# Norm sums inside the first FFN tile, and more Strassen tiles in layer 0

## The chip, the core and the metric

The kernel runs on one core of a Trainium2 chip. The metric is the device time of one execution in microseconds (us). A core has several engines that work side by side, each through its own queue, in order: PE (TensorE, matrix products), DVE (VectorE), ACT (ScalarE), POOL (GpSimd), and SP, which here issues nearly all loads. PE writes into PSUM, the others read it; operands lie in SBUF, in 128 partitions.

## The reference

A decoder trunk of two layers over 512 tokens with a model width of 1024. Each layer has a mixer, a cross-attention into 256 memory tokens, and a SwiGLU FFN of width 2816, each with an RMS norm before it and a residual add behind it. The change is in the FFN:

```python
def rms_norm(x, g):
    y = xf * lax.rsqrt(jnp.mean(xf * xf, axis=-1, keepdims=True) + RMS_EPS)
    return (y * g).astype(x.dtype)

def swiglu(h, w_gate_up, w_down):
    g, u = jnp.split(h @ w_gate_up, 2, axis=-1)
    return (jax.nn.silu(g) * u) @ w_down

x = x + swiglu(rms_norm(x, ffn_norm[layer]), ffn_w_gate_up[layer], ffn_w_down[layer])
```

## The kernel before

**Layout and precision.** Activations lie transposed: features in the partitions, the 512 tokens (T) along the free axis; a 1024-wide activation is eight such tiles (KD = 8). Float32 accuracy comes from splitting each operand into a high and a low part (`split`, L156 on ACT for the high part, L157 on DVE for the low; with a per-feature gain L159 and L160). A product is three matmuls, high by high, high by low and low by high (`mm3`, L169 to L171). Weights come in raw blocks by DMA (L93) and are split on ACT (L101) and DVE (L102); there are two raw buffers and three each of high and low.

**The FFN** (`ffn`) goes through the 2816 hidden features in 22 tiles f0 to f21 of 128, in parts of 4, 4, 4, 4 and 6 tiles. A *plain* tile makes its gate and up products with 48 matmuls of 512 columns (8 feature tiles x 3 x 2). A *fast* tile uses a Strassen form over two halves of the features and two halves of the tokens: seven products of 4 feature tiles, 84 matmuls of 256 columns. It needs sums and differences of half tiles of the normed features (`TA`, `TB`; L797 to L800, split into `ta` and `tb`) and sums of weight blocks, made by DVE from raw blocks `gr` and split into `sw`. f4 to f15 are fast in both layers. The down products of a part (8 of them, 12 matmuls each) run two per tile during the next part; those of the last part follow at the end. Gate and up of a plain tile go to the PSUM banks `mm` and `att`, sums and broadcasts to `tr`, down products to `s`; each has two buffers.

**The norm at the FFN's front.** During the cross-attention's output projection every finished tile of x is scaled by the norm's gain and split (`xg`), and its square is added to `ssq` on POOL (L250). The first two tiles f0 and f1 take `xg`, that is features without the norm's factor. Then four times two small matmuls with a column of ones sum `ssq` over the features (L186, `rstd_cols`); a short chain on DVE (L195, L220 to L223) and POOL (L219) makes the reciprocal root, DVE spreads it over a diagonal (L231), one matmul broadcasts it to all partitions (L233) and ACT copies it to R (L239). f0 and f1 are multiplied by R behind their products (L890, L892). From f2 on the products take the normed features `xn` = x times gain times R (L791), split by L156 and L157. In the code `normed` makes two of these, their half sums and the splits of both, four times.

**Last part and key scaling.** Before f16 the pool of the fast tiles is closed, and its memory is free for others. In layer 0, `aside` runs behind f17: it scales and splits the keys of the memory for the next layer (`mg`, eight times L159 on ACT and L160 on DVE).

**Order.** The program is written in the order of the code, and a scheduler then decides for each engine the order of its instructions, from a timing model and the dependences. `tc.issue_after(ins)` adds an order without a wait: what is inside comes behind `ins` on its engine.

Of the kernel before, what the change touches and what calls it, by code (L numbers as in the profile page):

```python
# [9 lines left out]
F32 = mybir.dt.float32  # L10
F32R = mybir.dt.float32r
# [3 lines left out]
ALU = mybir.AluOpType  # L15
# [3 lines left out]
P = 128  # L19
T = 512  # L20
D = 1024
KD = D // P
NT = T // P
# [9 lines left out]
DFF = 2816  # L33
NF = DFF // P
FFN_PARTS = (4, 4, 4, 4, 6)
FAST = range(4, 16)
HT = T // 2
KH = KD // 2
WARM = 12
EPS = 1e-6  # L40
PADW = 16
# [65 lines left out]
class Trunk:  # L107
# [128 lines left out]
    def norm_row(self, ssq, dim):  # L236
        ps = self.bcast(self.rstd_cols((ssq, dim, NT, None))[0])
        R = self.rp.tile([P, T], F32, name=self.nm("R"), tag="R")
        self.nc.scalar.copy(R, ps)  # L239
        return R  # L240

# [15 lines left out]
        return {"side": side, "gain": gain, "off": off, "ssq": self.new_ssq(), "xg": []}  # L257

    def feed(self, nxt, m, x=None):
        x = self.x[m] if x is None else x  # L260
        if nxt["gain"] is not None:
            h, l = self.pair(nxt["side"])
            self.split(x, h, l, scale=self.vec(nxt["gain"], nxt["off"] + m))
            nxt["xg"].append((h, l))
        self.add_square(nxt["ssq"], x, m == 0)

    def linear(self, W, blk, xs, off=0, bank="mm", ps=None, k0=0, k1=None):

# [163 lines left out]
    def even(self, nrm, nxt_spec):  # L432
# [4 lines left out]
        with ExitStack() as ctx:  # L437
# [20 lines left out]
            nc.scalar.activation(sq[2], z[2], AF.Square)  # L458
            R = self.rp.tile([P, T], F32, name=self.nm("R"), tag="R")
            ups = [self.linear(Win, 0, xg, bank="s", k1=3)]  # L460
# [4 lines left out]
            with tc.issue_after(self.mm_ins):  # L465
                row = self.bcast(rx)
            nc.scalar.copy(R, row)
            Rk = self.tmp("t1")
# [6 lines left out]
            kr = self.tmp("t0")  # L475
            nc.vector.tensor_mul(kr[rr], z[3][rr], R[rr])
            ta, tb = self.tmp("t1"), self.tmp("t1")
# [283 lines left out]
    def ffn(self, layer, nrm, nxt_spec, aside=None):  # L761


        nc, ins = self.nc, self.ins
        xg, A = nrm["xg"], nrm["side"]
        B = 1 - A
        final = nxt_spec is None
# [4 lines left out]
        Wg = Weights(self, ins["ffn_gu"], f"gu{layer}")  # L772
        lo, hi = slice(0, HT), slice(HT, T)
        xn, TA, TB = [None] * KD, [], []

        def products(f, xs):
            pg = self.linear(Wg, (layer * NF + f) * 2, xs, bank="mm")
            return pg, self.linear(Wg, (layer * NF + f) * 2 + 1, xs, bank="att")

        def hidden(u):  # L780
            h, l = self.pair(A)
            self.split(u, h, l)
            return h, l

        def normed(st):

            for k in range(KH):
                g = []
                for m in (k, k + KH):
                    t = self.inp.tile([P, T + PADW], F32, name=self.nm("xn"), tag="in")[:, :T]  # L790
                    nc.vector.scalar_tensor_tensor(t, self.x[m], self.vec(nrm["gain"], nrm["off"] + m), R,  # L791
                                                   op0=ALU.mult, op1=ALU.mult)
                    xn[m] = self.pair(B)
                    self.split(t, *xn[m])
                    g.append(t)
                a, b = self.tmp("t2"), self.tmp("t2")
                nc.vector.tensor_sub(a[:, lo], g[0][:, lo], g[0][:, hi])  # L797
                nc.vector.tensor_sub(a[:, hi], g[1][:, hi], g[0][:, hi])
                nc.vector.scalar_tensor_tensor(b[:, lo], a[:, lo], -1.0, g[1][:, hi], op0=ALU.mult, op1=ALU.subtract)
                nc.vector.scalar_tensor_tensor(b[:, hi], b[:, lo], -1.0, g[1][:, lo], op0=ALU.mult, op1=ALU.subtract)  # L800
                for src, lst, n in ((a, TA, "ta"), (b, TB, "tb")):
                    p = tuple(st.tile([P, T], F32R, name=self.nm(n), tag=f"{n}{i}{k}", bufs=1) for i in "hl")
                    self.split(src, *p)
                    lst.append(p)
# [53 lines left out]
        def plain(f):  # L858
            pg, pu = products(f, xn)
            t, u = self.tmp("t0"), self.tmp("t1")  # L860
            nc.scalar.activation(t, pg, AF.Silu)
            nc.vector.tensor_mul(u, pu, t)
            return hidden(u)

        def down(p, hs):
            nf = FFN_PARTS[p]
            W = Weights(self, ins[f"ffn_down{p}"], f"dn{layer}_{p}")
            n = D // (nf * P)
            return [lambda m=m: self.linear(W, layer * (KD // n) + m // n, hs, off=m % n * nf * P, bank="s")
                    for m in range(KD)]  # L870

        todo, f0, nxt = [], 0, None
        fastp = ExitStack()
        st = fastp.enter_context(self.tc.tile_pool(name=f"fast{layer}", bufs=1))
        for p, nf in enumerate(FFN_PARTS):
            last = p == len(FFN_PARTS) - 1
            if last:
                fastp.close()
                if final:
                    pool = self.ctx.enter_context(self.tc.tile_pool(name="tail", bufs=1))  # L880
                    into = [pool.tile([P, KD, nf * P], F32R, name=f"tail{i}", tag=f"tail{i}") for i in "hl"]
                    Wd = Weights(self, ins[f"ffn_down{p}"], f"dn{layer}_{p}", into=into)
            hs = []
            if p == 0:

                us, ps = [], [products(f, xg) for f in range(2)]
                R = self.norm_row(nrm["ssq"], D)
                for pg, pu in ps:
                    t, u = self.tmp("t0"), self.tmp("t1")
                    nc.vector.tensor_mul(t, pg, R)  # L890
                    nc.scalar.activation(t, t, AF.Silu)
                    nc.vector.tensor_mul(u, pu, R)  # L892
                    nc.vector.tensor_mul(u, u, t)
                    us.append(u)
                normed(st)
                hs += [hidden(u) for u in us]
            for f in range(f0 + len(hs), f0 + nf):
                hs.append(fast(f, st) if f in FAST else plain(f))
                if last and aside and f == f0 + 1:
                    aside()  # L900
                for _ in range(2):
                    if todo:
                        m = KD - len(todo)
                        self.residual(m, todo.pop(0)())
            f0 += nf
            if not last:
                todo = down(p, hs)
        if final:
            self.tail(Wd, hs, layer * KD, B)
            return None  # L910
        nxt = self.next_norm(B, *nxt_spec)
        for m, run in enumerate(down(p, hs)):
            self.residual(m, run(), nxt)
# [305 lines left out]
```

## Time and profile before

| | |
|---|---|
| median of 3 runs | 1443.02 us (1440.71 to 1443.83) |
| the profiled execution | 1440.62 us |
| its span, first to last instruction | 1438.8 us |
| mean granted TensorE clock | 0.985 |
| ACT busy, share of the span | 646.3 us, 45% |
| POOL busy, share of the span | 129.4 us, 9% |
| moved by DMA, mean rate | 139.38 MB, 97 GB/s |

The span lies 1.8 us inside the profiled execution's time. A timeline row gives the start, the duration, the engine, the line of the kernel, the operation, output <- inputs, the shape, the number of instructions in the row, and in brackets how long the engine was idle before it and what released it. Neighbouring matmuls overlap, so their cost is read from the distance of their starts. A windows row gives busy time of each engine in a stretch of the span. The granted clock is a share of full speed.

### The profile page before, as it was taken

The page shows a single profiled execution, that of the slowest core. Times are in us where ns is not written, and L with a number is a line of the kernel's source. Part 1 is how long each engine was busy: PE and PEld are TensorE (multiplying, and loading weights), DVE is VectorE, ACT ScalarE, POOL GpSimd, SP SyncE. Part 2 cuts the span into 40 slices and gives each one's busy share as a digit, 9 for nine tenths or more (in the row PEclk, how much of TensorE's full clock was granted, in tenths as well). Part 3 has the DMA queues.
Part 4 walks back from the last instruction along what each step waited for, and adds up shares of the span by engine and source line. Part 5 has one row for each costly group of instructions (what it writes and reads, how often), then busy time and mean ns, then how long its engine had stood idle before and what let it go on. Part 6 is the DMA issues. An engine that isn't in the chain of part 4 may idle for free.

```text
span 1438.8 us, 18665 instructions
## 1 busy us (share of the span) xinstructions
PE 1378.4 (96%) x7352; PEld 1172.8 (82%) x7352; DVE 887.0 (62%) x1404; ACT 646.3 (45%) x1034; POOL 129.4 (9%) x136
## 2 busy tenths in 40 slices
PE   9899999999699999999999989999987999999998
PEld 7678788878489889988888878887875898898887
DVE  6787664465676777644478695446638767764343
ACT  6478643443344434532444754335425444343231
POOL 0431031012000000000120002111210000000002
PEclk9999999999899999999999999999998999999999
DMA  6222162342123232222332234223430232313331
GB/s 214 82 78 73 54 190 74 103 146 89 58 74 95 97 104 87 74 93 91 102 103 88 89 114 145 93 75 103 145 102 30 88 103 89 116 46 103 102 103 60
DMA packets 44969, 139.38 MB, mean 97 GB/s; under 512 B 5584, under 2 KB 9808, under 8 KB 44880
## 3 DMA queue, kind: packets, MB, share of 16 engines
q1 hardware_dynamic: 43440, 136.86, 29.2%
q10 hardware_dynamic: 1440, 1.32, 0.3%
q8 instruction: 58, 0.95, 0.3%
q14 instruction: 31, 0.25, 0.1%
HBM read 135.93 MB, written 2.10 MB: 96 GB/s over the span
## 4 chain that ended last, share of the span: by engine, by line
PE 59%; DVE 6%; ACT 4%; issue 2%; DMA 1%; POOL 0%; POOLq 0%; DVEq 0%; ACTq 0%
PE mm L169 9%; PE mm L170 9%; PE mm L171 9%; PE s L171 5%; PE att L170 5%; PE s L169 5%; PE s L170 5%; PE att L169 5%; PE att L171 5%; ACT sw_h L156 1%; DVE act L157 1%; DMA gr<-in_ffn_gu_dram 1%; ACT t L850 1%; PE tr L169 1%; PE tr L170 1%
## 5 line engine op out<-in xcount | busy, mean ns | idle before, releaser
L250 POOL TENSOR_TENSOR ssq<-ssq,t 128x512 f32<-128x512 f32 (+1 forms) x42 | 67.9, 1617 | 644.5 <-issue 330.2
L169 PE MATMUL s<-act,dn_h 128*128 128x512 f32 x304 | 118.7, 390 | 0.0
L170 PE MATMUL s<-act,dn_h 128*128 128x512 f32 x304 | 118.4, 390 | 0.0
L171 PE MATMUL s<-act,dn_l 128*128 128x512 f32 x304 | 116.6, 397 | 0.1
L101 ACT CAST gu_h<-gu_raw 128x1024 fp32r<-128x1024 f32 x40 | 42.1, 1052 | 134.0 <-PE mm L170 75.9
L277 DVE TENSOR_TENSOR x<-s,x 128x512 f32<-128x512 f32 x72 | 49.6, 689 | 64.7 <-PE s L171 64.5
L102 DVE TENSOR_TENSOR gu_l<-gu_raw,gu_h 128x1024 fp32r<-128x1024 f32 x40 | 49.0, 1225 | 63.4 <-ACT gu_h L101 59.6
L156 ACT CAST sw_h<-sa 128x1024 fp32r<-128x1024 f32 x24 | 25.2, 1050 | 115.3 <-PE s L170 115.3
L169 PE MATMUL mm<-act,gu_h 128*128 128x512 f32 x160 | 64.5, 403 | 9.6 <-ACT act L156 9.6
L101 ACT CAST dn_h<-dn_raw 128x1024 fp32r<-128x1024 f32 (+1 forms) x40 | 40.3, 1008 | 68.9 <-PE s L170 33.2
L170 PE MATMUL mm<-act,gu_h 128*128 128x512 f32 x160 | 64.2, 401 | 6.8 <-DVE act L157 6.8
L171 PEld LDWEIGHTS s<-act,dn_l 128*128 128x128 f32 x304 | 57.0, 188 | 14.4 <-DVE dn_l L102 2.7
L170 PEld LDWEIGHTS s<-act,dn_h 128*128 128x128 f32 x304 | 57.0, 188 | 11.4
L169 PEld LDWEIGHTS s<-act,dn_h 128*128 128x128 f32 x304 | 57.2, 188 | 10.5 <-DVE x L277 0.3
L171 PE MATMUL att<-act,gu_l 128*128 128x512 f32 x160 | 62.9, 393 | 1.1 <-DVE gu_l L102 1.1
L169 PE MATMUL att<-act,gu_h 128*128 128x512 f32 x160 | 63.4, 396 | 0.1
L171 PE MATMUL mm<-act,gu_l 128*128 128x512 f32 x160 | 63.4, 396 | 0.0
L170 PE MATMUL att<-act,gu_h 128*128 128x512 f32 x160 | 62.8, 392 | 0.0
L171 PE MATMUL mm<-tb,sw_l 128*128 128x256 f32 x192 | 54.4, 284 | 0.0
L170 PE MATMUL mm<-tb,sw_h 128*128 128x256 f32 x192 | 54.4, 283 | 0.0
L169 PE MATMUL mm<-tb,sw_h 128*128 128x256 f32 x192 | 53.9, 280 | 0.0
L849 DVE TENSOR_TENSOR t<-att,pc 128x256 f32<-128x256 f32 x24 | 10.2, 424 | 66.7 <-PE att L171 66.7
(478 smaller groups left out, 4315.6 us busy)
## 6 DMA issues: line engine op xcount, KB each, us to landing
gr<-in_ffn_gu_dram SPq DMA_DIRECT2D x48, 512.0 KB, 3.8
gu_raw<-in_ffn_gu_dram SPq DMA_DIRECT2D x40, 512.0 KB, 3.5
dn_raw<-in_ffn_down_dram SPq DMA_DIRECT2D x32, 512.0 KB, 3.5
xk_raw<-in_xa_w_k_dram SPq DMA_DIRECT2D x16, 512.0 KB, 3.5
xq_raw<-in_xa_w_q_dram SPq DMA_DIRECT2D x16, 512.0 KB, 3.5
xv_raw<-in_xa_w_v_dram SPq DMA_DIRECT2D x16, 512.0 KB, 3.5
xo_raw<-in_xa_w_o_dram SPq DMA_DIRECT2D x16, 512.0 KB, 3.6
odin_raw<-in_od_w_in_dram SPq DMA_DIRECT2D x16, 512.0 KB, 3.5
```

The lines of the kernel that those rows point to most:

```text
L101: nc.scalar.copy(hi, src)
L102: self.low.tensor_sub(lo, src, hi[:, :].bitcast(F32))
L156: nc.scalar.copy(hi, src)
L157: nc.vector.tensor_sub(lo, src, hi.bitcast(F32))
L169: nc.tensor.matmul(out, wh, xh, start=begin and i == 0, stop=False, **kw)
L170: nc.tensor.matmul(out, wh, xl, start=False, stop=False, **kw)
L171: self.mm_ins = nc.tensor.matmul(out, wl, xh, start=False, stop=end and i == last, **kw).ins
L250: (low or nc.gpsimd).tensor_add(ssq[:, :n], ssq[:, :n], sq[:, :n])
L277: self.nc.vector.tensor_add(self.x[m], ps, self.x[m] if src is None else src)
L849: nc.vector.tensor_add(t[:, hi], Z, c[:, hi])
L850: nc.scalar.activation(t, t, AF.Silu)
```

## The change

Four things, and the diff cut to them:

1. **Front of both FFNs.** The norm sums are issued behind f0's gate product, the broadcast behind f0's up product, f1's products behind the broadcast. The eight normed features are made and split in one go (`normed`), the half sums after that (`halves`). The unsplit normed features now lie in the four buffers `sraw`, which also hold the raw weight blocks `gr` of the fast tiles.
2. **Which tiles are fast.** Layer 1: f5 to f15 (before f4 to f15). Layer 0: f5 to f21; its fast pool is closed behind f21.
3. **The key scaling** runs behind f21, before the last eight down products.
4. **The last square** of each norm (m = 7) is added by DVE instead of POOL.

```diff
--- before.py
+++ after.py
@@ -33,7 +33,7 @@
 DFF = 2816
 NF = DFF // P
 FFN_PARTS = (4, 4, 4, 4, 6)
-FAST = range(4, 16)
+FAST = range(5, 16), range(5, 22)
 HT = T // 2
 KH = KD // 2
 WARM = 12
@@ -257,12 +257,13 @@
         return {"side": side, "gain": gain, "off": off, "ssq": self.new_ssq(), "xg": []}
 
     def feed(self, nxt, m, x=None):
+        nc = self.nc
         x = self.x[m] if x is None else x
         if nxt["gain"] is not None:
             h, l = self.pair(nxt["side"])
             self.split(x, h, l, scale=self.vec(nxt["gain"], nxt["off"] + m))
             nxt["xg"].append((h, l))
-        self.add_square(nxt["ssq"], x, m == 0)
+        self.add_square(nxt["ssq"], x, m == 0, nc.vector if m == KD - 1 else None)
 
     def linear(self, W, blk, xs, off=0, bank="mm", ps=None, k0=0, k1=None):
 
@@ -761,7 +762,7 @@
     def ffn(self, layer, nrm, nxt_spec, aside=None):
 
 
-        nc, ins = self.nc, self.ins
+        nc, ins, tc = self.nc, self.ins, self.tc
         xg, A = nrm["xg"], nrm["side"]
         B = 1 - A
         final = nxt_spec is None
@@ -784,15 +785,19 @@
 
         def normed(st):
 
-            for k in range(KH):
-                g = []
-                for m in (k, k + KH):
-                    t = self.inp.tile([P, T + PADW], F32, name=self.nm("xn"), tag="in")[:, :T]
-                    nc.vector.scalar_tensor_tensor(t, self.x[m], self.vec(nrm["gain"], nrm["off"] + m), R,
-                                                   op0=ALU.mult, op1=ALU.mult)
-                    xn[m] = self.pair(B)
-                    self.split(t, *xn[m])
-                    g.append(t)
+            gs = [st.tile([P, 2, T], F32, name=self.nm("xn"), tag="sraw", bufs=4) for _ in range(KH)]
+            for m in range(KD):
+                t = gs[m % KH][:, m // KH, :]
+                nc.vector.scalar_tensor_tensor(t, self.x[m], self.vec(nrm["gain"], nrm["off"] + m), R,
+                                               op0=ALU.mult, op1=ALU.mult)
+                xn[m] = self.pair(B)
+                self.split(t, *xn[m])
+            return gs
+
+        def halves(st, gs):
+
+            for k, g in enumerate(gs):
+                g = g[:, 0, :], g[:, 1, :]
                 a, b = self.tmp("t2"), self.tmp("t2")
                 nc.vector.tensor_sub(a[:, lo], g[0][:, lo], g[0][:, hi])
                 nc.vector.tensor_sub(a[:, hi], g[1][:, hi], g[0][:, hi])
@@ -874,30 +879,37 @@
         st = fastp.enter_context(self.tc.tile_pool(name=f"fast{layer}", bufs=1))
         for p, nf in enumerate(FFN_PARTS):
             last = p == len(FFN_PARTS) - 1
-            if last:
+            if last and final:
                 fastp.close()
-                if final:
-                    pool = self.ctx.enter_context(self.tc.tile_pool(name="tail", bufs=1))
-                    into = [pool.tile([P, KD, nf * P], F32R, name=f"tail{i}", tag=f"tail{i}") for i in "hl"]
-                    Wd = Weights(self, ins[f"ffn_down{p}"], f"dn{layer}_{p}", into=into)
+                pool = self.ctx.enter_context(self.tc.tile_pool(name="tail", bufs=1))
+                into = [pool.tile([P, KD, nf * P], F32R, name=f"tail{i}", tag=f"tail{i}") for i in "hl"]
+                Wd = Weights(self, ins[f"ffn_down{p}"], f"dn{layer}_{p}", into=into)
             hs = []
             if p == 0:
 
-                us, ps = [], [products(f, xg) for f in range(2)]
-                R = self.norm_row(nrm["ssq"], D)
-                for pg, pu in ps:
+                pg = self.linear(Wg, layer * NF * 2, xg, bank="mm")
+                with tc.issue_after(self.mm_ins):
+                    cols = self.rstd_cols((nrm["ssq"], D, NT, None))[0]
+                with tc.issue_after(self.sum_ins):
+                    ps = [(pg, self.linear(Wg, layer * NF * 2 + 1, xg, bank="att"))]
+                with tc.issue_after(self.mm_ins):
+                    row = self.bcast(cols)
+                R = self.rp.tile([P, T], F32, name=self.nm("R"), tag="R")
+                nc.scalar.copy(R, row)
+                with tc.issue_after(self.row_ins):
+                    ps.append(products(1, xg))
+                for i, (pg, pu) in enumerate(ps):
                     t, u = self.tmp("t0"), self.tmp("t1")
                     nc.vector.tensor_mul(t, pg, R)
                     nc.scalar.activation(t, t, AF.Silu)
                     nc.vector.tensor_mul(u, pu, R)
                     nc.vector.tensor_mul(u, u, t)
-                    us.append(u)
-                normed(st)
-                hs += [hidden(u) for u in us]
+                    if i == 0:
+                        gs = normed(st)
+                    hs.append(hidden(u))
+                halves(st, gs)
             for f in range(f0 + len(hs), f0 + nf):
-                hs.append(fast(f, st) if f in FAST else plain(f))
-                if last and aside and f == f0 + 1:
-                    aside()
+                hs.append(fast(f, st) if f in FAST[not final] else plain(f))
                 for _ in range(2):
                     if todo:
                         m = KD - len(todo)
@@ -908,6 +920,9 @@
         if final:
             self.tail(Wd, hs, layer * KD, B)
             return None
+        fastp.close()
+        if aside:
+            aside()
         nxt = self.next_norm(B, *nxt_spec)
         for m, run in enumerate(down(p, hs)):
             self.residual(m, run(), nxt)
```

Three places show how the order moves; names ending in a number are the n-th tile of that name.

PE at the front of layer 0's FFN, before: the last matmuls of f1's up product (`att`, from features `act` and weights `gu`), the sums, the broadcast, then f2's gate (`mm`) and up (`att`) products on normed features.

```order
L169 MATMUL att_3616<-act_631_3506,gu_h_3612 128x512
L170 MATMUL att_3616<-act_632_3507,gu_h_3612 128x512
L171 MATMUL att_3616<-act_631_3506,gu_l_3613 128x512
L186 MATMUL tr_3641<-ones,ssq_3202 128x1 x4
L233 MATMUL tr_3661<-t_643_3656,ones 128x512
L169 MATMUL mm_3795<-act_651_3679,gu_h_3791 128x512
L169 MATMUL att_3826<-act_651_3679,gu_h_3822 128x512
```

The same in the change: the end of f0's gate product, the sums, and the start of f0's up product; then the end of that up product, the broadcast and the start of f1.

```order
L171 MATMUL mm_3523<-act_631_3506,gu_l_3520 128x512
L186 MATMUL tr_3548<-ones,ssq_3202 128x1 x4
L169 MATMUL att_3569<-act_604_3235,gu_h_3565 128x512
L170 MATMUL att_3569<-act_605_3236,gu_h_3565 128x512
L171 MATMUL att_3569<-act_604_3235,gu_l_3566 128x512
```

```order
L170 MATMUL att_3569<-act_632_3507,gu_h_3565 128x512
L171 MATMUL att_3569<-act_631_3506,gu_l_3566 128x512
L233 MATMUL tr_3599<-t_641_3594,ones 128x512
L169 MATMUL mm_3609<-act_604_3235,gu_h_3605 128x512
```

Sums and broadcast, which stood side by side behind 96 products, have 24 products between them and 48 of f1 behind them.

DVE in the same place, before, from the products with R on (`xn` the normed features, L157 the low halves of splits, L797 to L800 the half sums):

```order
L791 SCALAR_TENSOR_TENSOR xn_3709<-x,vecs,R_3663 128x512
L893 TENSOR_TENSOR t_647_3666<-t_647_3666,t_646_3665 128x512
L893 TENSOR_TENSOR t_649_3672<-t_649_3672,t_648_3671 128x512
L797 TENSOR_TENSOR t_656_3689<-xn_3677 128x256
L798 TENSOR_TENSOR t_656_3689<-xn_3683,xn_3677 128x256
L157 TENSOR_TENSOR act_652_3680<-xn_3677,act_651_3679 128x512
L157 TENSOR_TENSOR act_655_3686<-xn_3683,act_654_3685 128x512
L157 TENSOR_TENSOR act_664_3706<-xn_3703,act_663_3705 128x512
L157 TENSOR_TENSOR act_667_3712<-xn_3709,act_666_3711 128x512
L157 TENSOR_TENSOR act_699_3782<-t_647_3666,act_698_3781 128x512
L799 SCALAR_TENSOR_TENSOR t_657_3690<-t_656_3689,xn_3683 128x256
```

And in the change, behind the eight scalings (L802 to L805 are the half sums, L903 the second tile's product with R, L102 a weight split):

```order
L906 TENSOR_TENSOR t_647_3666<-t_647_3666,t_646_3665 128x512
L802 TENSOR_TENSOR t_674_3729<-xn_3671 128x256
L157 TENSOR_TENSOR act_653_3677<-xn_3671,act_652_3676 128x512
L157 TENSOR_TENSOR act_655_3682<-xn_3672,act_654_3681 128x512
L903 TENSOR_TENSOR t_670_3719<-mm_3609,R_3601 128x512
L157 TENSOR_TENSOR act_657_3687<-xn_3673,act_656_3686 128x512
L803 TENSOR_TENSOR t_674_3729<-xn_3671 128x256
L102 TENSOR_TENSOR gu_l_3819<-gu_raw_3816,gu_h_3818 128x1024
L157 TENSOR_TENSOR act_659_3692<-xn_3674,act_658_3691 128x512
L157 TENSOR_TENSOR act_661_3697<-xn_3671,act_660_3696 128x512
L157 TENSOR_TENSOR act_663_3702<-xn_3672,act_662_3701 128x512
```

The feature splits now stand nearly in a row; of the half sums only the first two subtractions (L802, L803) stand among them, the rest behind.

ACT at the end of layer 0's FFN in the change (`dn` are down weights, act_1103 is the high half of f21's hidden tile, sp_u belongs to the next layer's mixer); before, the `mg` rows stood behind f17:

```order
L101 CAST dn_4_h_6842<-dn_4_raw_6840 128x768
L159 ACTIVATE mg_6758<-keys_6753,vecs 128x256 x8
L949 ACTIVATE sp_u<-vecs 128x8
L156 CAST act_1103_6745<-t_1102_6651 128x512
```

The key scaling now stands ahead of f21's hidden tile. In the built program its first instruction waits for f21's last product, in whose pool's memory `mg` lies. PE has 13 down matmuls there before it takes act_1103.

## The prediction

> **What bounds the kernel now.** I read the page's busy shares and slices first, then TensorE's timeline around the first layer's FFN front, then the windows that cut this stretch up, then the rows of VectorE (DVE), ScalarE (ACT) and GpSimd (POOL) inside it.
>
> ```profile
> PE 1378.4 (96%) x7352; PEld 1172.8 (82%) x7352; DVE 887.0 (62%) x1404; ACT 646.3 (45%) x1034; POOL 129.4 (9%) x136
> PEclk9999999999899999999999999999998999999999
> ```
>
> TensorE is busy for 96% of the span, so the end is set by how many matmuls there are and by the few places where PE waits or runs at a lower clock. The clock row dips twice, in slices 11 and 31 (a slice is 36 us): behind 360 and 1080 us, in the two FFN fronts.
>
> ```profile
> 348.66 0.39 PE L169 MATMUL mm<-act,gu_h 128*128 128x512 f32 x1
> 348.89 0.39 PE L170 MATMUL mm<-act,gu_h 128*128 128x512 f32 x1
> 370.42 0.95 PE L186 MATMUL tr<-ones,ssq 128*128 128x1 f32 x8
> 375.45 1.92 PE L233 MATMUL tr<-t,ones 128*128 128x512 f32 x2 [4.08 <-DVE t L231]
> 381.87 0.79 PE L169 MATMUL mm<-act,gu_h 128*128 128x512 f32 x1 [4.50 <-ACT act L156]
> 385.68 0.79 PE L170 MATMUL mm<-act,gu_h 128*128 128x512 f32 x1 [2.17 <-DVE act L157]
> 395.97 0.50 PE L170 MATMUL mm<-act,gu_h 128*128 128x512 f32 x1 [1.13 <-DVE act L157]
> 407.10 0.50 PE L171 MATMUL att<-act,gu_l 128*128 128x512 f32 x1 [0.53 <-DVE gu_l L102]
> 437.73 0.39 PE L169 MATMUL s<-act,dn_h 128*128 128x512 f32 x1
> ```
>
> The first row is f0's first gate matmul. 96 wide matmuls (512 columns) take it to the norm sums at 370.42, so one costs 21.76/96 = 0.2267 us (also the step from the first row to the second). Then PE waits 4.08 us for the norm's row, 4.50 and 2.17 us for the first normed features, 1.13 for another. The last row is where f5, the second Strassen tile, has six of its seven products done. I use 348.66 to 437.73 as **the front**; both kernels do the same mathematics in it.
>
> ```profile
> 348.66:437.73 89.07, 75.27 (x383) 61.63 (x382) 55.59 (x94) 36.72 (x53) 3.73 (x2) 0.92 0.20 65
> 1050.59:1139.66 89.07, 75.56 (x383) 62.10 (x382) 55.40 (x93) 36.62 (x53) 3.72 (x2) 0.90 0.20 65
> 375.40:381.90 6.50, 1.95 (x3) 0.41 (x3) 3.88 (x7) 3.79 (x6) 0.00 (x0) 0.51 0.01 6
> 381.90:389.20 7.30, 5.13 (x11) 3.60 (x12) 7.30 (x14) 3.64 (x6) 0.00 (x0) 0.50 0.00 1
> 389.20:397.00 7.80, 6.16 (x24) 4.09 (x23) 7.80 (x17) 3.77 (x7) 0.00 (x0) 1.00 0.00 0
> ```
>
> Columns after the stretch and its length: busy us and instructions of PE, its weight loads, DVE, ACT, POOL, then the granted clock. Each layer's front takes 89.07 us. After the 4 us wait the clock stands at 0.51 and 0.50 up to 389.2, and DVE has no free moment from 381.9 to 397: there the front is DVE's.
>
> **The fronts.** The same work in the new order, counted out: f0 to f4 are now plain (f4 was fast), 5 x 48 = 240 wide matmuls; the two pending down products before the end point add 24; f5's six products are 72 narrow ones. Their prices:
>
> ```profile
> 460.07 0.28 PE L169 MATMUL mm<-tb,sw_h 128*128 128x256 f32 x1
> 469.54 0.29 PE L171 MATMUL mm<-ta,sw_l 128*128 128x256 f32 x1
> 730.57 0.95 PE L186 MATMUL tr<-ones,ssq 128*128 128x1 f32 x8
> 731.38 0.48 PE L169 MATMUL mm<-act,odin_h 128*128 128x512 f32 x1
> 731.70 0.39 PE L170 MATMUL mm<-act,odin_h 128*128 128x512 f32 x1
> 736.92 1.02 PE L233 MATMUL tr<-t,ones 128*128 128x512 f32 x2
> 737.38 0.79 PE L169 MATMUL att<-act,odin_h 128*128 128x512 f32 x1
> 738.01 0.40 PE L170 MATMUL att<-act,odin_h 128*128 128x512 f32 x1
> ```
>
> The first two are the ends of a run of 80 narrow matmuls (256 columns): 9.47/79 = 0.12 us each. The others show the recurrent stage, where sums and broadcast already stand between products with no wait: from the sums to the second matmul behind them 1.13 us, less one step of 0.227, is 0.90; for the broadcast 1.09 less 0.227 is 0.86. So without waits the front is 264 x 0.2267 + 72 x 0.12 + 0.90 + 0.86 = 59.85 + 8.64 + 1.76 = **70.25 us**, 18.8 less. That f4 turned plain (48 x 0.2267 = 10.88 against 84 x 0.12 = 10.08) is inside.
>
> Are there waits? Four covers have to hold.
>
> ```profile
> 350.86 0.75 DVE L160 SCALAR_TENSOR_TENSOR act<-x,vecs,act 128x512 fp32r<-128x512 f32 x1
> 350.98 1.79 POOL L250 TENSOR_TENSOR ssq<-ssq,t 128x512 f32<-128x512 f32 x1 [3.66 <-ACT t L249]
> 371.65 1.95 POOL L219 TENSOR_TENSOR sm<-sm,mhalf 128x4 f32<-128x4 f32 x1 [18.88 <-DVE sm L195]
> 374.43 0.87 DVE L231 TENSOR_SCALAR t<-ident,sm 128x128 f32<-128x128 f32 x4
> 377.40 0.59 ACT L239 COPY R<-tr 128x512 f32<-128x512 f32 x1 [5.96 <-PE tr L233]
> 378.02 0.69 DVE L890 TENSOR_TENSOR t<-mm,R 128x512 f32<-128x512 f32 x1 [2.72 <-ACT R L239]
> 380.42 2.73 DVE L791 SCALAR_TENSOR_TENSOR xn<-x,vecs,R 128x512 f32<-128x512 f32 x4
> 384.95 2.49 DVE L157 TENSOR_TENSOR act<-xn,act 128x512 fp32r<-128x512 f32 x4
> 357.43 1.22 DVE L102 TENSOR_TENSOR gu_l<-gu_raw,gu_h 128x1024 fp32r<-128x1024 f32 x1 [5.82 <-ACT gu_h L101]
> ```
>
> (1) *The sums* now stand 24 matmuls in, at 354.1. The last add was on POOL and ended at 352.77; on DVE, behind the split that ends at 351.61, it takes about 0.69 (the price of an f32 product of that size, L890) and ends at 352.3. Margin 1.8; the old place would also have made it. At the other norms this edit is worth 0 to 0.7 us each by the same rows, and I count nothing.
> (2) *The broadcast* waited 4.08 with an idle PE; 24 up matmuls, 5.44 us, now lie over that chain. Margin 1.4. Behind the waiting matmul stands all of f1, so an overrun costs PE its full length.
> (3) *The features.* Broadcast ends near 361.3, R near 362.0 (0.59). Then DVE has t and u of f0 (0.6 each in sequence), eight scalings (2.73/4 = 0.68 each), u's product: to 369.5; then, with one weight split (1.22), the second tile's t and a few half-width subtractions between, eight feature splits (0.62 each). The first comes near 370.5, the fourth near 374.5, the last near 378.8. PE finishes f1 at 372.2 and takes gate and up of f2 feature by feature: it wants the first at 372.6, the fourth at 377.2, the last at 382.8. The tightest is the low half of f2's up weights, wanted 14 matmuls in, at 375.3, with 0.9 to spare. Each 0.6 us that DVE falls behind there costs PE up to that.
> (4) *The half sums* (moved past f2, to f2, f3 and f4) must be ready for f5. From R to f4's end I count about 41 us of DVE work in 42.6. Margin 0.7 to 1.0 at f5's first split weights.
>
> ```profile
> gr<-in_ffn_gu_dram SPq DMA_DIRECT2D x48, 512.0 KB, 3.8
> ```
>
> The raw weights of f5 and f6 share their four buffers with the normed features now, so on SP's queue their loads move behind the half sums: f6's second waits until about 401.8 and lands 3.8 later. DVE idles some 2 us for it, in a stretch where PE has plain products.
>
> With margins this thin I allow 0.5 us of waits a front (bounds 0 and 5): 18.3 gained each, **-36.6** for two. The clock then has no 4 us wait to fall after.
>
> **The end of layer 0.** f16 to f21 become fast.
>
> ```profile
> 453.66:582.39 128.73, 127.63 (x866) 116.31 (x865) 91.44 (x136) 55.09 (x81) 0.00 (x0) 1.00 0.28 91
> 605.24:670.56 65.32, 65.32 (x290) 54.05 (x289) 32.73 (x61) 23.59 (x33) 0.00 (x0) 1.00 0.32 105
> 606.49 3.31 ACT L159 ACTIVATE mg<-keys,vecs 128x256 fp32r<-128x256 f32 x8
> 607.76 3.25 DVE L160 SCALAR_TENSOR_TENSOR mg<-keys,vecs,mg 128x256 fp32r<-128x256 f32 x8
> ```
>
> The first row is eight fast tiles with their down products, 16.09 each; the second four plain ones, 16.33. By counts a fast one saves 10.88 - 10.08 = 0.80; six save 4.8. But 24 wide downs and 84 narrow are 5.44 + 10.08 = 15.52, so a fast period carries 0.57 of small waits. Only four of the six have down products beside them (f16 to f19): +2.3. f20 and f21 run back to back with weight buffers reused sooner; no row shows two fast tiles without downs between, so between 0 and 2 us, and I take 0.5, near the steady 0.57.
>
> The memory-key scaling (eight on ACT, 3.31, eight on DVE, 3.25) did not hold PE before (65.32 busy of 65.32), so removing it there gains nothing. Now it waits for f21's last product, because it lies in memory freed by the fast tiles. Behind it on ACT are a small activation (0.2) and the high split (0.6) of f21's hidden tile; PE has 13 down matmuls, 2.95 us, before it wants that split. ACT gives it after 3.31 + 0.2 + 0.6, about 4.2; DVE, with two half-width products first, gives the low part near 0.85 + 3.25 + 0.68 plus handover, about 5.0 to 5.3. PE, using the high part for two matmuls meanwhile, waits about **1.9 us** (0 if f21's split went first, 3 if all hangs on DVE). Sum: -4.8 + 2.3 + 0.5 + 1.9 = **-0.1**, bounds -3 and +4.
>
> The Trainium skill, "TensorE: Matmul & The Clock Gate", section "Back-to-back issue gap", gives an isolated warm matmul N/2.4 + 2.5 ns, which is 215.8 for 512 columns and 109.2 for 256. By it, as an estimate, a fast tile would save 1.19 and not 0.80, and the four that are gained on balance 1.5 us more. The rows (226.7 and 120) disagree, and they are what the sum uses.
>
> **Sum.** 1440.62 (the profiled execution) - 36.6 - 0.1 = 1403.9. The median of the runs shown is 2.4 above that execution, so 1406.
>
> **Rivals.**
> *A, DVE becomes the bound of the second tile or of f5.* For it: 7.80 busy of 7.80 before, 41 of 42.6 by my count. If eight features and the half sums slip by 10% of 41, PE waits 4 us a front, 8 in all: 1411 to 1417. Against: the feature margins are over 1 us for most.
> *B, layer 0's end is dearer.* The key scaling holds both engines, or the wait halves the clock. 4.08 us did; 1.13 at 395.97 did not (1.00 granted); 1.9 lies between. Half clock for the 13.8 us that it lasted in the front costs up to 6.9: 1410 to 1415. The Trainium skill's same page, "What's actually happening", puts the drop at an idle window of about 3.4 us, by which 1.9 leaves the clock alone. The trace's 4.08 agrees, and nothing here shows a wait between.
> *C, the raw weight loads.* If f5's loads, not only f6's, come late by a landing of 3.8 us, two tiles a front wait: up to 7.6 each, 1414 to 1421. Against: half sums end some 10 us before f5.
> *D, slower than before.* If the broadcast still waits 4 us, because the DVE chain runs behind weight splits, the clock falls to 0.5 ahead of f1, and each wide matmul costs 0.2267 more for as long as it stays. The old front kept it 13.8 us. It decides from 83 matmuls (18.8/0.2267) in each front on; all 192 of f1 to f4 would give 43.5 a front, near 1490. It needs 5.4 us more in a chain that took 4.08.
> *E, the change does not do what it says.* The built order has sums and broadcast on either side of f0's up product, so only a wait at these places could undo it; that is D.
>
> **How the numbers follow.** Forecast 0.75 (1399 to 1411), A 0.12, B 0.07, C 0.03, D and E 0.03. The range 1400 to 1417 leaves out a little of the forecast below, most of C, and D. A measurement here can tell about 0.2%, 2.9 us: faster 0.96, same 0.015, slower 0.025.
>
> **What would show it.** Broadcast with no wait, clock 1.00 through both fronts, front about 70.7 us; f2's waits under 1 us; f16 to f19 near 16.1 each; about 1.9 us of wait ahead of the hidden tile of f21. A front of 75 or more says A; a gr landing just before f5's splits says C; a granted clock under 1 after f21 says B.

## The result, and the profile after

The change takes 1409.03 us (median of 4 runs, 1408.14 to 1410.87) against 1443.42 (1440.71 to 1444.9): ratio 0.9765, 95% interval 0.9748 to 0.9783, faster by 34.4 us. 1406 was predicted, 1400 to 1417 the range. The profiled execution took 1408.14 us, its span is 1406.3, so it lies 32.5 below the span before; the prediction's sum was 36.7.

The busy shares and the clock by slices, from the page of the change:

```profile
PE 1368.2 (97%) x7496; PEld 1176.1 (84%) x7496; DVE 910.8 (65%) x1449; ACT 652.7 (46%) x1053; POOL 119.3 (8%) x131
PEclk9989999999999999999999999999999999999999
```

Both dips of the clock at the fronts are gone. The 8 in the third slice is in the attention: in both kernels' windows the clock granted from 60 to 80 us is 0.74. PE's timeline at layer 0's front, and the windows of both fronts with the columns of before:

```profile
351.69 0.39 PE L169 MATMUL mm<-act,gu_h 128*128 128x512 f32 x1
357.13 0.50 PE L186 MATMUL tr<-ones,ssq 128*128 128x1 f32 x4
363.47 1.02 PE L233 MATMUL tr<-t,ones 128*128 128x512 f32 x2
375.23 0.39 PE L169 MATMUL mm<-act,gu_h 128*128 128x512 f32 x1
421.93 0.39 PE L169 MATMUL s<-act,dn_h 128*128 128x512 f32 x1
423.95 0.39 PE L169 MATMUL mm<-act,sw_h 128*128 128x256 f32 x1 [0.94 <-ACT sw_h L156]
```

```profile
351.69:421.93 70.24, 70.24 (x347) 59.45 (x346) 54.59 (x92) 32.68 (x47) 1.95 (x1) 1.00 0.34 113
1036.14:1106.39 70.25, 70.25 (x347) 59.46 (x346) 54.70 (x92) 32.64 (x47) 1.94 (x1) 1.00 0.34 112
```

No row from the first gate matmul to f5's sixth product has a bracket: PE is busy for 70.24 of 70.24 us at full clock, where it was 75.27 of 89.07. The count without waits was 70.25. Behind the end point stands a wait of 0.94 that I come back to.

DVE's rows over the features, and the two PE rows that used them most closely:

```profile
366.90 5.38 DVE L791 SCALAR_TENSOR_TENSOR xn<-x,vecs,R 128x512 f32<-128x512 f32 x8
373.13 1.29 DVE L157 TENSOR_TENSOR act<-xn,act 128x512 fp32r<-128x512 f32 x2
375.87 1.22 DVE L102 TENSOR_TENSOR gu_l<-gu_raw,gu_h 128x1024 fp32r<-128x1024 f32 x1
380.36 0.69 DVE L157 TENSOR_TENSOR act<-xn,act 128x512 fp32r<-128x512 f32 x1
406.89 0.69 DVE L828 TENSOR_TENSOR sa<-gr 128x512 f32<-128x512 f32 x1 [1.54 <-DMA gr<-in_ffn_gu_dram]
```

```profile
375.68 0.39 PE L170 MATMUL mm<-act,gu_h 128*128 128x512 f32 x1
378.40 0.39 PE L171 MATMUL att<-act,gu_l 128*128 128x512 f32 x1
```

The first low half ends near 373.8 and is used at 375.68, 1.9 us later; the weight split ends at 377.09 and is used at 378.40, 1.3 later; the last low half ends at 381.05. f6's raw weights let DVE idle for 1.54 us, and PE does not notice.

The end of layer 0's FFN, from f21's last product on:

```profile
679.85 0.84 ACT L101 CAST dn_h<-dn_raw 128x768 fp32r<-128x768 f32 x1 [4.71 <-PE mm L170]
680.59 3.30 ACT L159 ACTIVATE mg<-keys,vecs 128x256 fp32r<-128x256 f32 x8
680.72 0.96 DVE L102 TENSOR_TENSOR dn_l<-dn_raw,dn_h 128x768 fp32r<-128x768 f32 x1
681.93 3.25 DVE L160 SCALAR_TENSOR_TENSOR mg<-keys,vecs,mg 128x256 fp32r<-128x256 f32 x8
683.90 0.60 ACT L156 CAST act<-t 128x512 fp32r<-128x512 f32 x1
684.55 0.50 PE L169 MATMUL s<-act,dn_h 128*128 128x512 f32 x1 [1.63 <-ACT act L156]
685.10 0.68 DVE L157 TENSOR_TENSOR act<-t,act 128x512 fp32r<-128x512 f32 x1
685.83 0.50 PE L170 MATMUL s<-act,dn_h 128*128 128x512 f32 x1 [0.55 <-DVE act L157]
687.52 0.50 PE L169 MATMUL s<-act,dn_h 128*128 128x512 f32 x1 [0.48 <-DVE x L278]
```

PE waits three times: for the high half of f21's hidden tile behind the key scaling on ACT, for its low half behind the scaling on DVE, and for a residual add that is late behind both. On each engine a piece of down weights (`dn`) is split ahead of the scaling. By distances of starts (less a step of 0.227 per matmul) they cost 1.79 + 0.83 + 0.66 = 3.3 us.

The table cuts the span at f0's first matmul, the end of the front, the first pending down product in f15's period, and the next mixer's first product.

| stretch | before | after | difference | predicted |
|---|---|---|---|---|
| start to layer 0's front | 348.66 | 351.69 | +3.0 | 0 |
| front of layer 0 | 89.07 | 70.24 | -18.8 | -18.3 |
| f5 to f15 | 160.40 | 161.41 | +1.0 | 0 |
| **end of layer 0's FFN** | 127.00 | 128.81 | +1.8 | -0.1 |
| layer 1 up to its front | 325.46 | 323.99 | -1.5 | 0 |
| front of layer 1 (from 1050.59, 1036.14) | 89.18 | 70.25 | -18.9 | -18.3 |
| the rest | 299.03 | 299.91 | +0.9 | 0 |

### The profile page after: what moved, and what is told of

It reads as the page before. It is cut to its first block, busy times and chain, and to the rows that moved or that the text cites. A ratio compares the mean times of both kernels' runs of the same rounds, so it can differ in the third digit from the quotient of the medians.

```text
span 1406.3 us, 19022 instructions
## 1 busy us (share of the span) xinstructions
PE 1368.2 (97%) x7496; PEld 1176.1 (84%) x7496; DVE 910.8 (65%) x1449; ACT 652.7 (46%) x1053; POOL 119.3 (8%) x131
## 4 chain that ended last, share of the span: by engine, by line
PE 81%; ACT 7%; DVE 5%; issue 3%; DMA 2%; POOL 0%; POOLq 0%; DVEq 0%; ACTq 0%
PE mm L169 14%; PE mm L170 13%; PE mm L171 13%; PE s L171 6%; PE att L169 6%; PE att L170 6%; PE att L171 5%; PE s L169 5%; PE s L170 5%; ACT sw_h L156 2%; ACT dn_h L101 1%; ACT t L855 1%; PE tr L170 1%; PE tr L169 1%; PE tr L171 1%
## 5 line engine op out<-in xcount | busy, mean ns | idle before, releaser
L250 POOL TENSOR_TENSOR ssq<-ssq,t 128x512 f32<-128x512 f32 (+1 forms) x37 | 57.7, 1560 | 632.3 <-ACT t L249 632.0
L171 PE MATMUL mm<-tb,sw_l 128*128 128x256 f32 x224 | 63.5, 284 | 0.0
L170 PE MATMUL mm<-tb,sw_h 128*128 128x256 f32 x224 | 63.4, 283 | 0.0
L169 PE MATMUL mm<-tb,sw_h 128*128 128x256 f32 x224 | 62.8, 281 | 0.0
L102 DVE TENSOR_TENSOR gu_l<-gu_raw,gu_h 128x1024 fp32r<-128x1024 f32 x32 | 39.2, 1224 | 25.4 <-ACT gu_h L101 24.9
L157 DVE TENSOR_TENSOR sw_l<-gr,sw_h 128x1024 fp32r<-128x1024 f32 (+1 forms) x56 | 53.2, 950 | 1.1 <-ACT sw_h L156 0.8
L156 ACT CAST sw_h<-gr 128x1024 fp32r<-128x1024 f32 (+1 forms) x56 | 46.4, 828 | 15.4 <-PE mm L170 6.1
L169 PE MATMUL mm<-act,gu_h 128*128 128x512 f32 x128 | 50.3, 395 | 0.0
L169 PE MATMUL mm<-act,xq_h 128*128 128x512 f32 x128 | 50.1, 391 | 0.0
L171 PE MATMUL mm<-act,xq_l 128*128 128x512 f32 x128 | 50.1, 391 | 0.0
L169 PE MATMUL att<-act,gu_h 128*128 128x512 f32 x128 | 50.0, 390 | 0.0
```

Of the source, the lines that this page charges most:

```text
L102: self.low.tensor_sub(lo, src, hi[:, :].bitcast(F32))
L156: nc.scalar.copy(hi, src)
L157: nc.vector.tensor_sub(lo, src, hi.bitcast(F32))
L169: nc.tensor.matmul(out, wh, xh, start=begin and i == 0, stop=False, **kw)
L170: nc.tensor.matmul(out, wh, xl, start=False, stop=False, **kw)
L171: self.mm_ins = nc.tensor.matmul(out, wl, xh, start=False, stop=end and i == last, **kw).ins
```

## Experiments

**1. The parts apart.** First the front alone, with the end of layer 0 as before:

```diff
-FAST = range(5, 16), range(5, 22)
+FAST = range(5, 16), range(5, 16)
...
-            if last and final:
+            if last:
                 fastp.close()
+            if last and final:
...
                 hs.append(fast(f, st) if f in FAST[not final] else plain(f))
+                if last and aside and f == f0 + 1:
+                    aside()
...
-        fastp.close()
-        if aside:
-            aside()
```

> The change with its end of layer 0 undone (f16 to f21 plain again, the key scaling behind f17), the new front kept in both layers. My theory: the new front is the whole gain and the end of layer 0 costs 1.8 us, so both fronts stay at 70.2 us without waits, the stretch from f15's first pending down product to the next mixer's first product goes back from 128.8 to 127.0, and the time is about 1407 us (ratio to the kernel before about 0.975). Rival (the prediction's sum, where the end is worth -0.1): no difference from the changed kernel, 1409, and the stretch at 128.8 or 128.9.

1407.07 us (1405.87 to 1408.76), ratio 0.9758 (0.9738 to 0.9778). Windows row of its end stretch:

```profile
582.26:709.28 127.02, 127.02 (x566) 104.89 (x565) 62.93 (x100) 47.29 (x67) 9.17 (x6) 1.00 0.33 103
```

The stretch is the 127.00 of before. Then the end alone, in the kernel before:

```diff
-FAST = range(4, 16)
+FAST = range(4, 16), range(4, 22)
...
-                if last and aside and f == f0 + 1:
-                    aside()
...
+        fastp.close()
+        if aside:
+            aside()
         nxt = self.next_norm(B, *nxt_spec)
```

> The kernel before with only the end of layer 0 changed (f16 to f21 fast, the key scaling behind f21); f4 stays fast, the front as before. My theory: fronts at 89.1 us as before, the end's stretch from 127.0 to 128.8, time about 1445 us, ratio about 1.001. Rival (the prediction's sum): stretch 126.9, ratio 1.000. A ratio under 0.999 would say that the end gains by itself and loses only together with the front.

1443.88 us (1441.61 to 1445.99), ratio 1.0009 (0.9998 to 1.002). Its end stretch:

```profile
599.78:728.72 128.94, 125.09 (x782) 110.95 (x781) 94.02 (x156) 61.73 (x96) 9.01 (x6) 1.00 0.26 85
```

The end costs 1.9 us by itself and 1.8 beside the new front, and its rows have the same three waits (1.63, 0.56, 0.48). So the whole gain is the fronts', and the end of layer 0 gives some back. By total times 1.9 us is at the edge of what a measurement tells; the stretches tell it.

**2. The key scaling ahead of f21's hidden tile.** Ordered behind that tile's split on both engines (last_ins are the two instructions of the split):

```diff
...
-            aside()
+            with tc.issue_after(self.last_ins[0]), tc.issue_after(self.last_ins[1]):
+                aside()
```

> The changed kernel with the key scaling ordered behind the split of f21's hidden tile on ACT and DVE. My theory: the three waits there (1.63 for the high half, 0.55 for the low half, 0.48 for a residual) go, the stretch falls from 128.8 to about 126.3, the time to about 1406.5. Rival: the scaling only moves the wait, since its 3.3 us on DVE then delay the residual adds that free the down products' banks: the stretch stays above 128 and PE waits 2 us or more for DVE.

1404.59 us (1402.84 to 1406.65), ratio 0.9737 (0.9719 to 0.9756); stretch 580.94 to 707.44, 126.50. What is left of the waits, with the rows ahead of it:

```profile
678.23 0.60 ACT L156 CAST act<-t 128x512 fp32r<-128x512 f32 x1
678.74 3.30 ACT L159 ACTIVATE mg<-keys,vecs 128x256 fp32r<-128x256 f32 x8
680.07 2.06 DVE L160 SCALAR_TENSOR_TENSOR mg<-keys,vecs,mg 128x256 fp32r<-128x256 f32 x5
682.04 0.68 DVE L278 TENSOR_TENSOR x<-s,x 128x512 f32<-128x512 f32 x1
682.78 0.50 PE L169 MATMUL s<-act,dn_h 128*128 128x512 f32 x1 [0.97 <-DVE x L278]
```

2.3 us of the 3.3 go. The rival has a part in it: five scalings on DVE now stand ahead of the first residual add, and PE waits 0.97 for that.

**3. Where fast tiles pay in layer 0.** f20 and f21, which have no down products beside them, plain again:

```diff
-FAST = range(5, 16), range(5, 22)
+FAST = range(5, 16), range(5, 20)
...
                 hs.append(fast(f, st) if f in FAST[not final] else plain(f))
+                if last and not final and f == f0 + 3:
+                    fastp.close()
+                if last and aside and f == f0 + 4:
+                    aside()
...
-        fastp.close()
-        if aside:
-            aside()
```

> The changed kernel with f20 and f21 plain, the fast pool closed behind f19 and the key scaling behind f20, beside plain products. My theory: f16 to f19 at 16.02 us a tile gain 1.25 against plain ones, f20 and f21 cost what they did before, the stretch is 127.0 - 1.25 = 125.7, the time about 1406. Rival (fast tiles lose there whatever follows): 127 or more.

1405.98 us (1404.88 to 1406.67), ratio 0.9746 (0.973 to 0.9762); stretch 125.65 where 125.7 was expected. Beside the changed kernel on one chip, later:

> The version with the shortest end of layer 0 (f16 to f19 fast, f20 and f21 plain, key scaling behind f20) beside the changed kernel on one chip. My theory: 128.8 - 125.65 = 3.2 us faster than the changed kernel, some 1405 to 1406. Rival (the two differ by less than a measurement tells): within 1.5 us.

1405.52 us (1402.83 to 1406.97) against 1408.09 for the changed kernel. The stretches differ by 128.70 - 125.82 = 2.9 us and the medians by 2.6; the ratios to the kernel before overlap, 0.9752 (0.9738 to 0.9765) and 0.9766 (0.9753 to 0.9779). This version and that of experiment 2 are the two fastest here; which of them is faster the totals don't tell (its stretch is 0.85 us shorter).

**4. Which half of the new front carries the gain.** Placement alone: `normed` is that of before (two features, their half sums, the splits, four times; cut from the diff), and `halves` goes.

```diff
-                    if i == 0:
-                        gs = normed(st)
+                    if i == 0:
+                        normed(st)
...
-                halves(st, gs)
```

> The changed kernel with its normed features made as before, two at a time with their half sums between (in the old buffers); sums and broadcast stay on either side of f0's up product. My theory: the placement carries the gain. R is there 10 us before f2, DVE needs about 25 us from R to the last low half, and PE, which here takes three products on the first features, wants that half about 15 us into f2: fronts of 70.2 to 72.5 us, clock 1.00, waits of 0 to 2 us, total 1409 to 1413. Rival (half of the gain is in splitting all features first): the waits of 4.50, 2.17 and 1.13 us come back, about 8 us a front, fronts at 78, total about 1424.

1420.66 us (1420.41 to 1421.28), ratio 0.9851 (0.9836 to 0.9865); fronts of 75.44 and 75.90 us. Two of its waits at f2:

```profile
384.38 0.50 PE L169 MATMUL mm<-act,gu_h 128*128 128x512 f32 x1 [1.65 <-ACT act L156]
386.48 0.50 PE L170 MATMUL mm<-act,gu_h 128*128 128x512 f32 x1 [1.13 <-DVE act L157]
```

It fell between both expectations. I had let the last feature decide, but one in the middle was later against its use. The old `normed` makes the features in pairs (0 and 4, 1 and 5, 2 and 6, 3 and 7), and PE uses them from 0 to 7. By the count of its matmuls (27 from f2's first at 375.78 on, nine for each feature with those of f3's gate) it stands at feature 3 when it waits, and what it waits for is the seventh feature that DVE makes, whose scaling starts at 382.93. Then the split order alone, with sums and broadcast behind f1:

```diff
-                pg = self.linear(Wg, layer * NF * 2, xg, bank="mm")
...
-                    ps.append(products(1, xg))
+                ps = [products(f, xg) for f in range(2)]
+                R = self.norm_row(nrm["ssq"], D)
```

> The changed kernel with sums, chain and broadcast back behind f1's products; all eight features are still scaled and split ahead of the half sums. My theory: the 4.08 us wait and the half clock behind it return, and the first split now stands behind eight scalings, so PE waits 8 to 10 us for the first feature and little after it: front 86 to 91 us, total about 1442 (1438 to 1446), hardly faster than the kernel before. Rival (the order of features and half sums carries half of the gain): front about 80 us, total about 1425.

1442.37 us (1440.59 to 1445.45), ratio 1.0002 (0.9992 to 1.0012); fronts of 87.05 and 87.75.

```profile
377.98 2.05 PE L233 MATMUL tr<-t,ones 128*128 128x512 f32 x2 [4.08 <-DVE t L231]
383.33 0.80 PE L169 MATMUL mm<-act,gu_h 128*128 128x512 f32 x1 [3.31 <-ACT act L156]
387.92 0.79 PE L169 MATMUL mm<-act,gu_h 128*128 128x512 f32 x1 [3.37 <-DVE t L894]
390.06 0.79 PE L170 MATMUL mm<-act,gu_h 128*128 128x512 f32 x1 [1.34 <-DVE act L157]
```

The 4.08 is back, and 8.0 us of waits follow: for the first feature's high half (3.31), for a bank that DVE's product of f1 with R (L894) frees (3.37), and for that feature's low half (1.34). In layer 0's front the placement alone gives 13.6 of 18.8 us and the split order alone 2.0; on top of the placement it gives the other 5.2. With a late R it has nothing to work on. (All three have f4 plain, which costs 0.8 of each. "Split order" is two things, features made in the order of use and half sums kept behind them; no run parts these.)

**5. How near DVE is to being the bound.** Scalings into a scratch tile that nothing reads, ahead of the features, in each front (two, then range(6)):

```diff
                     if i == 0:
-                        gs = normed(st)
+                        z = self.tmp("t2")
+                        for _ in range(2):
+                            z_ins = nc.vector.scalar_tensor_tensor(z, self.x[0], self.vec(nrm["gain"], nrm["off"]), R,
+                                                                   op0=ALU.mult, op1=ALU.mult).ins
+                        with tc.issue_after(z_ins):
+                            gs = normed(st)
```

> The changed kernel with two more scalings of a feature into a scratch tile ahead of the features on DVE in each front: 2 x 0.66 = 1.3 us of work that nothing uses. My theory: the tightest row had 1.3 us to spare (a weight split that ended at 377.1, wanted at 378.4), so waits of 0 to 0.5 us a front, total unchanged within 1 us. Rival (DVE is the bound of the front, as rival A of the prediction has it): 1.3 us a front, 2.6 in all.

1410.13 us (2 runs), fronts 71.40 and 71.40: 1.15 us more each, nearer to the rival. PE waits 0.50 for a weight's high half on ACT, whose order had moved too.

> The same with six, 4.0 us of work, as much as the slip that rival A of the prediction names. Rival A: PE waits about 4 us a front, total about 1417. My theory: less. 1.3 us are spare, and the order that PE then takes (products of f3 on the first features) covers part of the rest: 0.5 to 2.5 us a front, total 1410 to 1414.

1425.91 us (2 runs), fronts 79.63 and 78.8: 9 us more each, beyond either expectation. Here the scheduler also put two weight splits, two products and a hidden tile's split (4.1 us) ahead of the first low half, so DVE was 8.7 us late for it and not 4. So a cleaner one, with the six ahead of all that uses R:

```diff
+                z = self.tmp("t2")
+                for _ in range(6):
...
+                with tc.issue_after(z_ins):
-                for i, (pg, pu) in enumerate(ps):
+                    for i, (pg, pu) in enumerate(ps):
...
```

> The changed kernel with six more scalings into a scratch tile on DVE in each front, now ahead of everything else that DVE does with R, so that the order behind them stays near that of the changed kernel. From the rows: R used at 365.7 (with f0 at 351.7), 6 x 0.66, t and u of f0 1.2, eight scalings 5.3, and by the built order t of f1, a weight split, u's product and half a sum (2.7) ahead of the first low half (0.6), which so ends at 379.5; PE wants it at 375.9. My theory (behind a slack of 1.9 us PE pays one to one): a wait of 3.6 us a front, one wait and hardly any behind it; total about 1416 if the clock holds, about 1421 if a wait of 3.6 us halves it for some 5 us. Rival (DVE slips are covered by products of f3): under 1.5 us a front, total under 1412.

1420.14 us (2 runs), fronts 77.06 and 76.10.

```profile
364.40 4.68 DVE L903 SCALAR_TENSOR_TENSOR t<-x,vecs,R 128x512 f32<-128x512 f32 x6
378.17 1.90 DVE L157 TENSOR_TENSOR act<-xn,act 128x512 fp32r<-128x512 f32 x3
376.33 0.47 PE L169 MATMUL mm<-act,gu_h 128*128 128x512 f32 x1 [1.80 <-DVE t L908]
378.91 0.80 PE L170 MATMUL mm<-act,gu_h 128*128 128x512 f32 x1 [2.11 <-DVE act L157]
```

```profile
374.00:379.00 5.00, 1.09 (x5) 0.39 (x3) 5.00 (x9) 4.20 (x7) 0.00 (x0) 0.82 0.12 28
379.00:384.30 5.30, 5.30 (x13) 4.20 (x14) 5.30 (x9) 0.62 (x1) 0.00 (x0) 0.53 0.28 88
```

PE waits 1.80 us for a bank that DVE's product of f1 with R (L908) frees and 2.11 for the first low half (3.6 expected in one), and behind that 13 matmuls run at a granted 0.53. The six scalings took 4.6 us (their starts lie 0.77 apart and not 0.66), and a product with R and a weight split stand ahead of the first low half that the changed kernel has behind it. So this half ends 28.5 us into the front where it was 22.1. Behind a slack of some 2 us DVE is the bound of f2: it is 6.4 us later, and the front is 5.9 to 6.8 longer, by the waits and then by the clock.

**6. The square on DVE.**

```diff
-        self.add_square(nxt["ssq"], x, m == 0, nc.vector if m == KD - 1 else None)
+        self.add_square(nxt["ssq"], x, m == 0, None)
```

> The changed kernel with the last square of every norm back on POOL. My theory: nothing. POOL's add would end 4.1 us into the front and the sums are wanted at 5.4; fronts 70.2 us, total as the changed kernel within 1 us (1408 to 1410). Rival: the new place of the sums has no margin for the 1.8 us add, and PE waits up to 1 us a front.

1408.19 us (1404.89 to 1410.05), fronts 70.25 and 70.24: nothing, as expected.

**7. The 3 us ahead of the first front.**

> The changed kernel once more, for the stretches that the change leaves alone. My theory: the half clock near 167 us (1.6 us) and the late weight load near 302 us (1.4 us) of its first profile were of that execution, not of the change: the stretch ahead of the first front is 348.7 to 351.7 us, fronts 70.2, end of layer 0 128.8, median between 1407 and 1410. Rival (the change delays something ahead of the front): again 351.5 or more, with both.

1408.09 us (1405.41 to 1408.25), fronts 70.25 and 70.25, end 128.70. Neither the dip of the clock nor the late load came back, and the first front still began at 351.15: my theory held for the two events and not for the sum. In the other twelve profiles it begins between 349.5 and 352.2, in 348.66 only in that of before; with the first stage as before it was 349.92 (the end alone) and 350.39 (experiment 6). In this one it is 2.7 us behind before's already at 47.7 us: 1.1 behind waits for the first weight loads and splits, and 1.6 through another fall of the clock (granted 0.51 from 43.0 to 46.5 us, where before has 1.00). So before's profile was at the short end of a spread of some 3 us, and what part of the 3.0 the change itself has, if any, stays open.

## Why the prediction was right, and where its sizes were off

- **What bounds the kernel, and the count of the front**: right. The stretch without waits was put at 70.25 and is 70.24 and 70.25; sums and broadcast cost what their rows in the recurrent stage said.
- **Cover 1, the sums** (margin 1.8, the old place of the add would do): right, shown by experiment 6. **Cover 2, the broadcast** (margin 1.4): no wait, clock 1.00; experiment 4 shows that its placement is most of the gain.
- **Cover 3, the features** (0.9 at the tightest): no wait, 1.3 measured. That the margin is real and thin is shown by experiment 5, and rival A's mechanism by it too. Its price, 4 us for 4 us of slip, is near what was paid (5.9 to 6.8 for 6.4), but by two parts that nearly cancel: the slack and PE's other work cover 2.5 of the slip, and what follows the waits at a lower clock adds 2.0 to 2.9.
- **Cover 4, half sums and raw loads**: right; DVE idles 1.54 us for a load (2 expected) and PE has other work. Rival C did not come.
- **The allowance of 0.5 us a front**: the waits inside are 0, but my end point hid one. Where the first fast tile hands over to the second PE waits some 0.9 us for `sw_h`, in the kernel before at 422.73, inside the stretch, and after the change at 423.95, behind it. f5 to f15 takes 1.0 us longer for it, so the real gain of a front is 17.8 to 18.0 against the 18.3 of the sum.
- **The end of layer 0** (-0.1; measured +1.8) is the term that was mis-sized. f16 to f19 were right: 647.41 - 583.34 = 64.07 for four, 1.25 below the plain ones' 65.32, where -0.9 was expected. The waits at f21's hidden tile were put at 1.9 and are 3.3. 2.6 of it is the tile itself: a down-weight cast of 0.84, which the order shown with the change already had ahead of the scaling on ACT, was left out of the count, and the low half came later because DVE splits the same weights (0.96) ahead of its scaling. The residual add behind, which I had not counted, cost the other 0.66. The small waits of f20 and f21 were put at 0.5 and sum to 1.4. It stayed inside the bounds of -3 to +4, and of rival B the dearer scaling happened and the lower clock did not (granted 1.00 from 684.5 to 712). The latter is in part luck: nine profiles have the first two of these waits, and in one of them, that of the placement experiment, the clock behind them is 0.50 from 692 to 695 us and the stretch 129.48. The prediction also says that nothing shows a wait between 1.13 and 4.08 us. The trace of before does: PE waits 2.53 us at 67.57 and 1.77 at 69.89, and the clock is 0.50 from 70 to 78 us.
- **The starting point.** The sum was made against an execution whose first stage was short; +3.0 there and -1.5 in layer 1 (a late weight load of the cross-attention that is in layer 1 before and in layer 0 after) are no part of the change that a run shows. From median to median 34.4 was gained where 36.7 was forecast, and the end of layer 0 alone is 1.9 of the 2.3 between them.

## What to carry to other kernels

In this kernel a norm's chain of small steps cost PE no wait once a product that doesn't need it stood between its sums and its broadcast, and once what it releases (eight features) was made in the order of use with the rest deferred; the one alone gave 13.6 and the other 2.0 us of 18.8. When work is moved behind a new last tile, walk the queue in which it lands: all that stands ahead of it and all that waits behind it, down to the adds that free the next bank. And choose the ends of a counted stretch so that the same hand-overs lie inside it in both kernels.

## What the runs showed of the hardware

The clock falls behind waits shorter than 4 us too, and not each time. All 14 profiles have the two waits near 70 us that are given above for before, with two small matmuls between, and a fall to 0.50 with them. In the placement experiment both fronts have the same two waits (1.65 and 1.13, three matmuls between them); PE's windows behind them in layer 0 and layer 1:

```profile
387.00:391.00 4.00, 4.00 (x19) 3.24 (x19) 4.00 (x10) 2.05 (x4) 0.00 (x0) 1.00 0.02 4
1077.90:1081.90 4.00, 4.00 (x12) 3.08 (x12) 4.00 (x10) 2.04 (x4) 0.00 (x0) 0.60 0.00 0
```

19 matmuls at a granted 1.00 in the one, 12 at 0.60 in the other. Behind the waits of 1.63 and 0.55 at f21 it stayed up in eight profiles of nine. It even falls where the timeline shows no wait: all profiles have a row of 22 sum matmuls (L186) of one column each near 40 us (2.4 us), and in five of them, the repeat of the changed kernel among them, the clock halves behind it. The Trainium skill, "TensorE: Matmul & The Clock Gate", section "What's actually happening", says that the gate looks at a window of about 3.4 us that runs freely, so that the moment of a change depends on where work falls in it. That two equal patterns end differently agrees with it; that PE was not idle throughout (three matmuls lie between, and the 22 short ones have no wait) shows that the window need not be empty. The same may be behind the dip at 166 to 172 us in the attention (granted 0.72, about 1.6 us), which 2 of 14 profiles have with the same instructions; that was not tried.
